# Issuing the strips of the index scores, and of their sums over heads, as one row per set

## The chip, the cores and the metric

The kernel runs on one core of one Trainium2 chip. The metric is the device time of one execution in microseconds (us). The engines that matter here are TensorE (PE in the profile, its weight loads PEld), VectorE (DVE), ScalarE (ACT), GpSimd (POOL) and SyncE (SP, which issues most of the DMAs).

## The reference

The program is one decoder layer over 512 prompt tokens and 8 sample sequences of 4 new tokens each: a SwiGLU block, a mixer (a gated convolution beside sparse attention), and a second SwiGLU block. The part in question is the indexer of the samples. For each sample it scores all 4096 cached keys, and the scores pick the 256 keys that attention may use:

```
def indexer_scores(qi, wi, ki):
    s = jax.nn.relu(jnp.einsum('bqhd,bsd->bqhs', qi, ki).astype(jnp.float32))
    return jnp.einsum('bqhs,bqh->bqs', s, wi.astype(jnp.float32)) * (D_IDX ** -0.5 * N_IDX_HEADS ** -0.5)
```

`qi` are the index queries (8 heads of 64), `ki` the cached index keys (64 wide), `wi` a weight for each head.

## The kernel before

All of it is written for one core with a tile framework. The Python code traces instructions, each with a priority; a scheduler then sets the order on each engine by these priorities and by its own estimate of when inputs are ready, and puts in the waits. Inside the mixer a planner interleaves generators ("A" and "B" for the index projections, "S" for the sample scores, "Q" and "K" for the other projections, "V" for the search of the threshold, "L" for raw logits, "D" for the prompt's top-k, and so on), and gives each a priority offset. After the second half of the first SwiGLU block ends at about 400 us, the mixer begins, and it ends at about 800 us; the second SwiGLU block follows.

`sample_scores` (generator S) does the indexer of the samples. It works in 8 steps n, 4 for each half jh of the keys; a step takes two samples (b2 = 0 and 1).

- `keys(n, b2)` gathers 512 KB of index keys into `kn` by an indirect DMA from POOL's queue (4 buffers, shared with the gathers of attention, `ckn`), and `key_transpose` turns them: 8 transposes on TensorE into the two PSUM banks of `KTp`, then one ACT copy into `kt`.
- `scores(n)` multiplies the queries with the two `kt`. There are four products (two halves of the columns, `hf`, by two samples, `b2`) of 512 columns. Each has 64 output rows, so the two samples write two strips of 64 partitions of one PSUM tile, `ssc`. ACT applies the ReLU and writes `Srel`, of which there are 4 buffers (n % 4).
- `gathered(jh, c)` runs when the four steps of a half are through, for each of two column halves c: four products `headsum` with 32 output rows each (one for each of the four `Srel` tiles) write four strips of 32 partitions of one PSUM tile, `SC`. ACT (for jh 0) or DVE (for jh 1) takes the sum to `sc`. The last step also scores the new tokens (`sxp`, `sxh`).

`KTp`, `ssc`, `sxp` and `sxh` share two PSUM buffers (tag "w", `wunit`), used in turn; `SC` has one buffer (tag "t").

When `sc` is complete, `sample_select` (generator V) searches the threshold with counts on DVE and ACT (tiles `flip`, `top`, `cand`). In the meantime TensorE works on projections (`nat`), keys and logits of attention and the convolution (`gc`, `hc`, `gb`).

All matmuls and transposes of the mixer go through the helpers `mm` (L134) and `tp` (L138), so these two lines carry most of TensorE's rows there. In the trace a float32 product has two MATMUL records: an "x2" is one strip.

Of the kernel before, what the change touches and what calls it, by code (L numbers as in the profile page):

```python
# [55 lines left out]
PINNED = 'BQK'  # L56
LGD = 2
KTB = 3
SB = 1
RSTEPS = 2  # L60
ZB = 1
# [60 lines left out]
class Trunk:  # L122
# [14 lines left out]
    def tp(self, *args):  # L137
        ins = self.nc.tensor.transpose(*args)  # L138
        return self.tc.keep_in_program_order(ins) if self.pin else ins

    def wunit(self, name):
        return self.ps.tile([128, 2, 512], F32, name=name, tag="w", bufs=2)
# [125 lines left out]
    def factors(self, srcs, nk):  # L268
# [13 lines left out]
        def parts(src, n):  # L282
            if n == 1:
                ts = [self.fp.tile([128, nk * 128], F32R, name=nm, tag=nm + "4", bufs=1) for nm in ("whi", "wlo")]
            else:
                slot, self.slot = self.slot, (self.slot + 1) % 3
                ts = [self.sp.tile([128, n * nk * 128], F32R, name=nm, tag=f"{nm}{slot}", bufs=1) for nm in ("whi", "wlo")]
            hi, lo = (t.rearrange("p (h k m) -> p h k m", h=n, k=nk) for t in ts)
            nc.scalar.activation(hi, src, AF.Copy)  # L289
            nc.vector.tensor_sub(lo, src, hi.bitcast(F32))  # L290
            return [(hi[:, h], lo[:, h]) for h in range(n)]

        p11, p12 = parts(st[0], 2)
        s12, s34 = (self.fp.tile([128, 2, nk, 128], F32, name=n, tag=n, bufs=SB) for n in ("s12", "s34"))
        for dst, a, b, op in ((s12[:, 0], a21, a22, ALU.add), (s12[:, 1], s12[:, 0], a11, ALU.subtract),
# [584 lines left out]
    def key_transpose(self, kn, name):  # L880
# [3 lines left out]
        for r in range(8):  # L884
            self.tp(wf[:, r * 128:(r + 1) * 128], kn[:, r * 128:(r + 1) * 128], self.ident)
        kt = self.ktp.tile([128, 1024], F32, name=name, tag="KT", bufs=KTB)
        self.nc.scalar.activation(kt, wf, AF.Copy)
        return kt

    def sample_scores(self, mp):  # L890

        nc = self.nc
        selb = mp.tile([128, 512], F32, name="selb", tag="flip", bufs=1)
        nc.gpsimd.tensor_copy(selb[:, 0:1], self.rn[:, 0:1])
        nc.scalar.dma_start(selb, self.i["c_late"])
        wm = mp.tile([128, 4, 2, 32], F32, name="wm")

        def head_weights():
            u = self.sunit("wsel")
            for bp in range(4):  # L900
                self.mm(u[:, bp * 8:(bp + 1) * 8], selb[:NS, bp * 128:(bp + 1) * 128], self.wi[:NS, 0, :],
                        start=True, stop=True)
            wt = mp.tile([128, 4, 8], F32, name="wt")
            nc.vector.tensor_mul(wt, u[:, :32].rearrange("p (a b) -> p a b", a=4), self.oneh[:, None, :].to_broadcast([128, 4, 8]))
            wc = mp.tile([128, 4], F32, name="wc")
            nc.vector.tensor_reduce(wc, wt, axis=AX.X, op=ALU.add)
            nc.gpsimd.memset(wm, 0.0)
            for bp in range(4):
                for jh in range(2):
                    nc.vector.tensor_scalar(wm[:, bp, jh, 16 * jh:16 * jh + 16], self.pat, wc[:, bp:bp + 1], None, op0=ALU.mult)  # L910

        def headsum(out, S, bp, jh):
            self.mm(out, wm[:, bp, jh, :], S, start=True, stop=True)

        sc = self.sc
        kts, SS = {}, {}

        def keys(n, b2):
            jh, bp = divmod(n, 4)
            b = 2 * bp + b2  # L920
            kn = self.gather(self.kvp, self.i["cache_idx_k"], 1024, self.ii[:, jh, b:b + 1], "kn", "kv", KV)
            kts[n, b2] = self.key_transpose(kn, "kt")

        def scores(n):
            bp = n % 4
            w = self.wunit("ssc")
            for hf in range(2):
                for b2 in range(2):
                    self.mm(w[64 * b2:64 * b2 + 64, hf, :], self.qbi[:, 2 * bp + b2].rearrange("p r t h -> p (r t h)"),
                            kts[n, b2][:, hf * 512:(hf + 1) * 512], start=True, stop=True)  # L930
            S = self.lgt(n % 4, "Srel")
            nc.scalar.activation(S, w.rearrange("p a b -> p (a b)"), AF.Relu)
            SS[bp] = S

        def gathered(jh, c):
            u = self.tunit("SC")
            for bp in range(4):
                headsum(u[32 * bp:32 * bp + 32, :], SS[bp][:, c * 512:(c + 1) * 512], bp, jh)
            dst = sc[:, 512 * c:512 * c + 512]
            if jh == 0:  # L940
                nc.scalar.activation(dst, u, AF.Copy, scale=IDX_SCALE)
            else:
                nc.vector.scalar_tensor_tensor(dst, u, IDX_SCALE, dst, op0=ALU.mult, op1=ALU.add)

        keys(0, 0)
        yield
        keys(0, 1)
        yield
        for n in range(8):
            if n == 2:  # L950
                head_weights()
            if n < 7:
                keys(n + 1, 0)
                yield
            if n == 4:
                gathered(0, 0)
                yield
                gathered(0, 1)
                yield
            scores(n)  # L960
            yield
            if n < 7:
                keys(n + 1, 1)
                yield
        sx = mp.tile([128, 4, NEXT], F32, name="sx")
        u = self.wunit("sxp")[:, 0, :]
        for bp in range(4):
            for b2 in range(2):
                self.mm(u[64 * b2:64 * b2 + 64, bp * NEXT:(bp + 1) * NEXT],
                                 self.qbi[:, 2 * bp + b2].rearrange("p r t h -> p (r t h)"), self.kix, start=True, stop=True)  # L970
        nc.scalar.activation(sx, u[:, :4 * NEXT].rearrange("p (a b) -> p a b", a=4), AF.Relu)
        u = self.wunit("sxh")[:, 0, :]
        for bp in range(4):
            headsum(u[32 * bp:32 * bp + 32, :NEXT], sx[:, bp, :], bp, 0)
        for c in range(2):
            yield
            gathered(1, c)
        ext = sc[:, NSEG:]
        nc.vector.scalar_tensor_tensor(ext, u[:, :NEXT], IDX_SCALE, self.valid, op0=ALU.mult, op1=ALU.mult)
        nc.vector.tensor_add(ext, ext, self.vfill)  # L980
# [719 lines left out]
```

## Time and profile before

| | |
|---|---|
| time, three runs | 1253.44, 1253.94, 1253.94 us; median 1253.94 |
| the profiled execution's own time | 1253.65 us, of which the span of the trace is 1251.9 us |
| granted TensorE clock, mean | 0.989 |
| TensorE busy, matmuls | 1192.6 us, 95% of the span |
| VectorE busy | 858.7 us, 69% |
| ScalarE busy | 544.2 us, 43% |
| GpSimd busy | 446.3 us, 36% |

The table is over the whole span, and stages with different limits lie in it. The products in question all lie between 425 and 475 us.

### The profile page before, as it was taken

Reading aid. Unit: us, or ns where it says so; the run is one execution under the profiler, and the core shown is the slowest. Engines: PE = TensorE matmul, PEld = TensorE weight load, DVE = VectorE, ACT = ScalarE, POOL = GpSimd, SP = SyncE. Lnnn points to the kernel's source line nnn. Section 1 sums busy time; section 2 is a strip of 40 time slices with the busy share of each in tenths; the row PEclk is TensorE's granted clock in tenths of the full one; section 3 lists DMA queues with packets and bytes.
Section 4 is the critical chain, followed back from the end, with each engine's and each line's share of the span. In section 5 each row is a group of like instructions: output and inputs, shape, how many; then the busy total and the mean of one; then the engine's idle time right before and its main releaser. Section 6 shows DMA issues by size and latency. Waiting matters only on the chain.

```text
span 1251.9 us, 22739 instructions
## 1 busy us (share of the span) xinstructions
PE 1192.6 (95%) x9216; PEld 1070.5 (86%) x9221; DVE 858.7 (69%) x1433; ACT 544.2 (43%) x830; POOL 446.3 (36%) x465
## 2 busy tenths in 40 slices
PE   8999999999999998899979999989989999999998
PEld 7999989999998747775667545779989999999998
DVE  6449998359965208999999753246997379845972
ACT  6224544134444455465534546335444134423432
POOL 2202651145302536665423222221650255204500
PEclk9999999999999998999998999999999999999999
DMA  8523224223331562245214544544223312432332
GB/s 239 140 68 105 73 86 134 86 69 90 94 104 59 168 199 85 65 139 169 66 58 142 163 135 140 164 136 135 77 60 110 110 55 86 123 93 71 95 86 75
DMA packets 184364, 136.08 MB, mean 109 GB/s; under 512 B 5706, under 2 KB 172434, under 8 KB 184260
## 3 DMA queue, kind: packets, MB, share of 16 engines
q1 hardware_dynamic: 171700, 91.62, 25.3%
q0 software_dynamic: 11904, 42.26, 10.5%
q8 instruction: 72, 1.18, 0.4%
q10 hardware_dynamic: 656, 0.76, 0.2%
q14 instruction: 32, 0.26, 0.1%
HBM read 131.66 MB, written 2.96 MB: 108 GB/s over the span
## 4 chain that ended last, share of the span: by engine, by line
PE 67%; DVE 22%; issue 5%; DMA 3%; ACT 2%; POOL 1%; DVEq 0%; ACTq 0%; POOLq 0%
PE Y L195 21%; PE U L372 10%; PE G L372 6%; DVE wlo L290 5%; PE Yo L134 3%; PE lg L134 3%; PE U L195 3%; PE nat L134 3%; PE KTp L138 3%; PE G L195 2%; DVE flip L1010 2%; DMA ckn<-in_cache_k,ik 1%; PE ssc L134 1%; DVE u L421 1%; PE O L134 1%
## 5 line engine op out<-in xcount | busy, mean ns | idle before, releaser
L297 POOL TENSOR_TENSOR s<-wst 128x512 f32<-128x512 f32 x68 | 98.2, 1448 | 363.7 <-DMA wst<-in_ffn_w_gate 209.0
L170 ACT ACTIVATE whi<-wst 128x1024 fp32r<-128x1024 f32 (+3 forms) x105 | 99.9, 957 | 203.9 <-PE Y L195 72.5
L195 PE MATMUL Y<-hl,whi 128*128 128x272 f32 (+2 forms) x704 | 147.8, 288 | 0.0
L195 PE MATMUL Y<-hh,whi 128*128 128x272 f32 (+2 forms) x704 | 147.6, 289 | 0.0
L195 PE MATMUL Y<-hh,wlo 128*128 128x272 f32 (+2 forms) x704 | 147.5, 288 | 0.0
L175 DVE TENSOR_TENSOR wlo<-wst,whi 128x1024 fp32r<-128x1024 f32 (+3 forms) x88 | 99.8, 1134 | 21.3 <-ACT whi L170 19.7
L195 PEld LDWEIGHTS Y<-hl,whi 128*128 128x128 f32 x704 | 111.5, 188 | 0.0
L195 PEld LDWEIGHTS Y<-hh,wlo 128*128 128x128 f32 x704 | 111.3, 188 | 0.0
L195 PEld LDWEIGHTS Y<-hh,whi 128*128 128x128 f32 x704 | 110.8, 188 | 0.0
L290 DVE TENSOR_TENSOR wlo<-wst,whi 128x1024 fp32r<-128x1024 f32 (+1 forms) x68 | 96.3, 1416 | 15.4 <-ACT whi L289 15.0
L509 DVE SCALAR_TENSOR_TENSOR x<-Y,x 128x544 f32<-128x544 f32 x46 | 33.2, 723 | 105.0 <-PE Y L195 105.0
L289 ACT ACTIVATE whi<-s 128x1024 fp32r<-128x1024 f32 x68 | 71.8, 1056 | 70.9 <-PE Y L195 29.8
L290 DVE TENSOR_TENSOR wlo<-s,whi 128x1024 fp32r<-128x1024 f32 x68 | 87.8, 1292 | 10.5 <-ACT whi L289 10.5
L372 PE MATMUL U<-xh,whi 128*128 128x272 f32 x272 | 78.5, 289 | 0.2 <-ACT m L375 0.2
L372 PE MATMUL G<-xh,wlo 128*128 128x272 f32 x272 | 78.4, 288 | 0.0
L372 PE MATMUL U<-xh,wlo 128*128 128x272 f32 x272 | 78.4, 288 | 0.0
L173 POOL TENSOR_TENSOR wlo<-wst,whi 128x1024 fp32r<-128x1024 f32 (+2 forms) x17 | 34.5, 2032 | 122.7 <-ACT whi L170 122.2
L372 PE MATMUL G<-xh,whi 128*128 128x272 f32 x272 | 78.3, 288 | 0.0
L372 PE MATMUL U<-xl,whi 128*128 128x272 f32 x272 | 78.1, 287 | 0.0
L372 PE MATMUL G<-xl,whi 128*128 128x272 f32 x272 | 78.1, 287 | 0.0
L289 ACT ACTIVATE whi<-wst 128x1024 fp32r<-128x1024 f32 (+1 forms) x68 | 57.2, 841 | 42.4 <-DMA wst<-in_ffn_w_gate 17.3
L372 PE MATMUL U<-x3h,wlo 128*128 128x272 f32 x204 | 61.4, 306 | 11.3 <-DVE wlo L290 11.3
(428 smaller groups left out, 3591.9 us busy)
## 6 DMA issues: line engine op xcount, KB each, us to landing
wst<-in_ffn_w_up SPq DMA_DIRECT2D x44, 512.0 KB, 4.3
wst<-in_ffn_w_gate SPq DMA_DIRECT2D x43, 512.0 KB, 3.8
wst<-in_ffn_w_down SPq DMA_DIRECT2D x32, 512.0 KB, 3.9
wst<-in_w_in SPq DMA_DIRECT2D x16, 512.0 KB, 3.7
wst<-in_ffn_w_down SPq DMA_DIRECT2D x16, 384.0 KB, 3.4
xin<-in_x_prompt SPq DMA_DIRECT2D x4, 512.0 KB
wst<-in_w_in SPq DMA_DIRECT2D x8, 256.0 KB, 4.9
wst<-in_w_out SPq DMA_DIRECT2D x8, 256.0 KB, 5.8
```

Source lines behind the costliest of these rows:

```text
L134: ins = self.nc.tensor.matmul(*args, **kw)
L138: ins = self.nc.tensor.transpose(*args)
L170: nc.scalar.activation(hi, st, AF.Copy)
L173: nc.gpsimd.tensor_tensor(lo, st, hi.bitcast(F32), op=ALU.subtract)
L175: nc.vector.tensor_sub(lo, st, hi.bitcast(F32))
L195: self.nc.tensor.matmul(unit[:, i, :c1 - c0], a[:, k, :], b[:, k, c0:c1], start=k == 0 and j == 0, stop=k == n - 1 and j == 2)
L289: nc.scalar.activation(hi, src, AF.Copy)
L290: nc.vector.tensor_sub(lo, src, hi.bitcast(F32))
L297: nc.gpsimd.tensor_tensor(dst, a, b, op=op)
L372: nc.tensor.matmul(out, w[:, k, :], b[:, k, :], start=k == 0 and j == 0, stop=k == nk - 1 and j == 2)
L509: nc.vector.scalar_tensor_tensor(xc, Y[:, :, :HT], 0.5, xc, op0=ALU.mult, op1=ALU.add)
L1010: V.tensor_scalar(junk, src, cand[:, k:k + 1], None, op0=ALU.is_ge, op1=ALU.add, accum_out=cnt[:, k:k + 1])
```

## The change

A new helper, `in_a_row`, takes the products of a set. It traces the one given first, and then the others with a priority raised by `RUN` and with an edge that keeps each of them behind the first on TensorE. In `scores` and in `gathered` the product that is given first is one that needs the tile that becomes ready last (`b2` = 1; the fourth `Srel`), so that the others have their inputs when it starts. Nothing is computed differently.

```
+RUN = 5000
...
+    def in_a_row(self, last, *others):
+
+
+        with self.tc.high_priority(offset=RUN):
+            with self.tc.issue_after(last().ins):
+                for f in others:
+                    f()
...
         def headsum(out, S, bp, jh):
-            self.mm(out, wm[:, bp, jh, :], S, start=True, stop=True)
+            return self.mm(out, wm[:, bp, jh, :], S, start=True, stop=True)
...
             w = self.wunit("ssc")
-            for hf in range(2):
-                for b2 in range(2):
-                    self.mm(w[64 * b2:64 * b2 + 64, hf, :], self.qbi[:, 2 * bp + b2].rearrange("p r t h -> p (r t h)"),
-                            kts[n, b2][:, hf * 512:(hf + 1) * 512], start=True, stop=True)
+
+            def part(hf, b2):
+                return lambda: self.mm(w[64 * b2:64 * b2 + 64, hf, :], self.qbi[:, 2 * bp + b2].rearrange("p r t h -> p (r t h)"),
+                                       kts[n, b2][:, hf * 512:(hf + 1) * 512], start=True, stop=True)
+            self.in_a_row(*[part(hf, b2) for hf in range(2) for b2 in (1, 0)])
...
             u = self.tunit("SC")
-            for bp in range(4):
-                headsum(u[32 * bp:32 * bp + 32, :], SS[bp][:, c * 512:(c + 1) * 512], bp, jh)
+            self.in_a_row(*[lambda bp=bp: headsum(u[32 * bp:32 * bp + 32, :], SS[bp][:, c * 512:(c + 1) * 512], bp, jh)
+                            for bp in (3, 0, 1, 2)])
```

The line numbers of the changed kernel are 1 to 10 higher (L134 becomes L135, L138 becomes L139). Three places show what the scheduler makes of it. First, TensorE after the second set of scores, in the kernel before (`ssc` scores, `SC` sums over heads, `KTp` transposes of keys, `qiT` and `kiT` transposes of the prompt's index queries and keys):

```order
L134 MATMUL ssc<-kt,qbi 64x512 x4
L138 MATMUL qiT<-main,nq 128x128 x2
L134 MATMUL SC<-Srel,wm 32x512
L138 MATMUL KTp<-main,kn 128x128 x8
L134 MATMUL SC<-Srel,wm 32x512
L138 MATMUL KTp<-main,kn 128x128 x8
L138 MATMUL kiT<-main,nk 128x128
L134 MATMUL ssc<-kt,qbi 64x512 x4
L138 MATMUL KTp<-main,kn 128x128 x8
L138 MATMUL qiT<-main,nq 128x128 x2
L138 MATMUL KTp<-main,kn 128x128 x2
L134 MATMUL SC<-Srel,wm 32x512
```

The same place in the changed kernel, a little further on:

```order
L135 MATMUL ssc<-kt,qbi 64x512 x4
L139 MATMUL KTp<-main,kn 128x128 x8
L139 MATMUL kiT<-main,nk 128x128
L135 MATMUL SC<-Srel,wm 32x512 x4
L139 MATMUL KTp<-main,kn 128x128 x8
L135 MATMUL ssc<-kt,qbi 64x512 x4
L139 MATMUL qiT<-main,nq 128x128 x2
L135 MATMUL nat<-wst,xs 32x256 x2
L135 MATMUL SC<-Srel,wm 32x512 x4
L139 MATMUL KTp<-main,kn 128x128 x16
L135 MATMUL ssc<-kt,qbi 64x512 x4
```

The four strips of the first sum stood one by one, each between transposes; now they follow each other behind the fourth set of scores. The second sum was a row of four already.

Second, TensorE at the end of the scores, in the kernel before (`sxp` and `sxh` are the scores and sums of the new tokens, `nat` and `natS` a projection of the samples):

```order
L134 MATMUL nat<-wst,xs 32x256 x4
L134 MATMUL ssc<-kt,qbi 64x512
L134 MATMUL SC<-Srel,wm 32x512
L134 MATMUL sxp<-kix,qbi 64x32
L134 MATMUL ssc<-kt,qbi 64x512
L134 MATMUL sxp<-kix,qbi 64x32
L134 MATMUL ssc<-kt,qbi 64x512
L134 MATMUL sxp<-kix,qbi 64x32
L134 MATMUL ssc<-kt,qbi 64x512
L134 MATMUL sxp<-kix,qbi 64x32 x5
L134 MATMUL natS<-part,main 32x256
```

And in the changed kernel:

```order
L139 MATMUL KTp<-main,kn 128x128 x8
L135 MATMUL nat<-wst,xs 32x256 x4
L135 MATMUL ssc<-kt,qbi 64x512 x4
L135 MATMUL sxp<-kix,qbi 64x32 x8
L135 MATMUL natS<-part,main 32x256
L139 MATMUL kiT<-main,nk 128x128
L135 MATMUL SC<-Srel,wm 32x512 x4
```

The last set of scores is a row of four, and so is the third sum, whose strips stood apart before. Of the eight sets of scores the first and the last were broken up before; of the four sums the first and the third.

Third, VectorE some 200 us later, where the order differs again: the rounds of the prompt's top-k (`MAX`, then `MATCH_REPLACE` on `pw`) stand beside work that frees PSUM for TensorE (`gc` of the convolution, and `P<-plg`, the prompt's softmax). Before:

```order
L1261 TENSOR_REDUCE rs<-sums 128x1
L1166 TENSOR_TENSOR gc<-gc,R_5251 128x272
L1122 MAX m_7652<-pw_4410 128x8
L1262 RECIPROCAL rs<-rs 128x1
L1123 MATCH_REPLACE pw_4410<-m_7652,pw_4410 128x256
L1122 MAX m_7655<-pw_4410 128x8
L1123 MATCH_REPLACE pw_4410<-m_7655,pw_4410 128x256
L1270 COPY px<-PxT 32x128
L1122 MAX m_7658<-pw_4410 128x8
L1123 MATCH_REPLACE pw_4410<-m_7658,pw_4410 128x256
L1349 ISA P,pmx<-plg,main 128x128
```

In the changed kernel:

```order
L1271 TENSOR_REDUCE rs<-sums 128x1
L1132 MAX m_7652<-pw_4410 128x8
L1272 RECIPROCAL rs<-rs 128x1
L1133 MATCH_REPLACE pw_4410<-m_7652,pw_4410 128x256
L1176 TENSOR_TENSOR gc<-gc,R_5251 128x272
L1132 MAX m_7655<-pw_4410 128x8
L1133 MATCH_REPLACE pw_4410<-m_7655,pw_4410 128x256
L1132 MAX m_7658<-pw_4410 128x8
L1133 MATCH_REPLACE pw_4410<-m_7658,pw_4410 128x256
L1280 COPY px<-PxT 32x128
L1132 MAX m_7661<-pw_4410 128x8
L1133 MATCH_REPLACE pw_4410<-m_7661,pw_4410 128x256
```

One more round of the top-k stands ahead of `gc` and of the first `P`; ahead of the third `P`, some fifteen rows on, it is one round and a `MAX` more. Between the second place and the third the order of VectorE is the same, and that of the other engines differs only in details.

## Rows read from the trace of the kernel before

**Rows 1.** Busy time by stretch; (x) counts instructions, PEclk granted clock.

```profile
core 0: us, PE busy (x) PEld busy (x) DVE busy (x) ACT busy (x) POOL busy (x), PEclk, DMA share, GB/s
425.28:475.00 49.72, 49.55 (x286) 23.71 (x285) 6.48 (x22) 28.28 (x39) 20.35 (x31) 1.00 0.57 171
482.00:660.00 178.00, 157.08 (x1075) 124.80 (x1075) 171.40 (x458) 90.13 (x148) 92.14 (x150) 0.96 0.32 97
```

**Rows 2.** Timeline, DVE and POOL: start, duration, instruction [idle before <- releaser].

```profile
471.22 0.61 POOL L756 TENSOR_TENSOR qsq<-nq 32x256 f32<-32x256 f32 x1 [4.96 <-ACT nq L842]
475.09 0.69 DVE L943 SCALAR_TENSOR_TENSOR sc<-SC,sc 128x512 f32<-128x512 f32 x1 [0.23 <-PE SC L134]
480.29 0.42 DVE L758 TENSOR_REDUCE qms<-qsq 128x4 f32<-128x256 f32 x1 [1.32 <-POOL qsq L756]
```

**Rows 3.** Timeline of PE: the sums, single strips and a row of four.

```profile
452.31 1.07 PE L134 MATMUL SC<-Srel,wm 128*32 128x512 f32 x8
453.30 2.26 PE L138 MATMUL KTp<-main,kn 128*128 128x128 f32 x16
455.49 1.04 PE L134 MATMUL SC<-Srel,wm 128*32 128x512 f32 x2
456.46 1.94 PE L134 MATMUL ssc<-kt,qbi 128*64 128x512 f32 x8
...
470.69 0.62 PE L134 MATMUL SC<-Srel,wm 128*32 128x512 f32 x1
...
471.72 0.39 PE L134 MATMUL nat<-whi,xh 128*128 128x256 f32 x1
```

**Rows 4.** Timeline of PE: the first set of scores, and the second.

```profile
425.28 1.08 PE L134 MATMUL ssc<-kt,qbi 128*64 128x512 f32 x4
...
429.62 0.24 PE L138 MATMUL kiT<-main,nk 32*128 32x32 f32 x1
...
431.87 1.09 PE L138 MATMUL KTp<-main,kn 128*128 128x128 f32 x8
432.89 1.94 PE L134 MATMUL ssc<-kt,qbi 128*64 128x512 f32 x8
434.76 0.44 PE L138 MATMUL qiT<-main,nq 128*128 128x128 f32 x2
```

**Rows 5.** Timeline of PE: the last set of scores.

```profile
463.95 1.09 PE L138 MATMUL KTp<-main,kn 128*128 128x128 f32 x8
...
465.54 1.07 PE L134 MATMUL ssc<-kt,qbi 128*64 128x512 f32 x2
466.54 1.04 PE L134 MATMUL SC<-Srel,wm 128*32 128x512 f32 x2
467.52 0.24 PE L134 MATMUL sxp<-kix,qbi 128*64 128x32 f32 x1
...
469.41 0.48 PE L134 MATMUL sxp<-kix,qbi 128*64 128x32 f32 x8
469.82 0.62 PE L134 MATMUL natS<-part,main 128*32 128x256 f32 x2
```

**Rows 6.** Timeline of ACT: copies of turned keys.

```profile
454.79 1.95 ACT L887 ACTIVATE kt<-KTp 128x1024 f32<-128x1024 f32 x2
...
465.14 1.02 ACT L887 ACTIVATE kt<-KTp 128x1024 f32<-128x1024 f32 x1 [0.60 <-PE KTp L138]
```

**Rows 7.** Timeline of DVE: one round of the prompt's top-k.

```profile
665.16 0.42 DVE L1122 MAX8 m<-pw 128x8 f32<-128x256 f32 x1
...
665.69 0.41 DVE L1123 MATCH_REPLACE8 pw<-m,pw 128x256 f32<-128x256 f32 x1
```

**Rows 8.** Timeline of PE at the wait behind those rounds.

```profile
673.10 0.39 PE L134 MATMUL hc<-xh,whi 128*128 128x272 f32 x1 [0.74 <-DVE pmx L1349]
```

**Rows 9.** Timeline of POOL: the last gather of index keys.

```profile
454.67 0.94 POOL L876 DMA_INDIRECT kn<-in_cache_idx_k,ii  x1 [3.71 <-PE KTp L138]
```

**Rows 10.** Chain that ended last: a gather that TensorE waited for.

```profile
700.74 5.30 DMA ckn<-in_cache_k,ik
```

## The prediction

> **What bounds the kernel now.** I looked first at the busy time by stretch, because the products of the change all lie in one of 50 us. From 425.28 to 475 us TensorE is busy for 49.55 of 49.72 us at the full clock, while VectorE has 6.5 us of work and ScalarE 28.3 [rows 1]. So TensorE is the limit there, and any time that its row of instructions gives up is worth looking for. From 482 to 660 us it is the other way round: VectorE is busy for 171.4 of 178 us, TensorE for 157 [rows 1]. That stretch begins with the search of the threshold, and the search needs the sums of the scores.
>
> Next I read how the one hands over to the other [rows 2]. VectorE takes the last sum at 475.09, but its first count of the search waits until 480.29 for something else too, a reduction `qms` that stands ahead of it in VectorE's queue and waits for POOL. POOL's part begins with `qsq` at 471.22, after 4.96 us of waiting for a copy of `natS`. `natS` is made by TensorE just before the last sums. Both ways into the search thus start from TensorE's end of this stretch, so that a gain there should pass to the search whole. To check that for POOL: with the sums done 6.3 us earlier, its chain would start 6.3 us earlier as well, since `natS` moves with them.
>
> Last I read TensorE's timeline product by product, to see what a strip costs. I count from one start to the next, because the durations overlap.
>
> **What a row saves.** A single strip of a sum holds TensorE from 455.49 to 456.46, 0.97 us. A row of four holds it from 452.31 to 453.30, 0.99 us [rows 3]. Four strips of 32 columns run side by side if nothing stands between them, and the three others are nearly free. The same is to be seen for two strips of scores: a record pair x2 and two strips x4 both last 1.07 to 1.08 us [rows 4, 5]. A whole set of scores in a row, four strips in two pairs, takes 432.89 to 434.76, 1.87 us, and eight transposes 431.87 to 432.89, 1.02 us [rows 4].
>
> The Trainium skill speaks against this in "TensorE: Matmul & The Clock Gate", Part 3, "What overlaps and what doesn't": weights of the next product load beside a running one only where the row groups differ. Strips of one set here differ in columns alone, so by that rule a row would be four strips one after another, some 3.9 us, and the change would give nothing. The trace disagrees with 0.99 us, but only for the rows that are there already, so I keep the rule as a rival.
>
> Now set by set, of those that the order shows broken up:
>
> - First scores: with the eight transposes that were mixed in, 425.28 to 429.62, 4.34 us [rows 4]. In rows 1.87 + 1.02 = 2.89. Saved 1.45.
> - First sum: four single strips at 0.97, 3.88 us. In a row 0.99. Saved 2.9. (The order has these four, each between transposes; one of them stands for all in rows 3.)
> - Third sum: three single strips, 2.91 us, and a fourth mixed with `sxh`, 470.69 to 471.72, 1.03 us [rows 3]. In a row 0.99, and `sxh` by itself at what eight records of `sxp` take, 469.41 to 469.82, 0.41 us [rows 5]. Saved 3.94 - 1.40 = 2.55.
> - Last scores with `sxp`: 465.54 to 469.82, 4.28 us, less the 0.98 of a sum's strip inside (466.54 to 467.52, counted above): 3.30 [rows 5]. In rows 1.87 + 2 x 0.41 = 2.69. Saved 0.6.
>
> Together 7.5 us. The other six sets of scores and the other two sums are rows already and save nothing.
>
> **What the rows cost.** A loose strip was also a filler: it stood where TensorE would have waited for ScalarE's copies. Three such waits come to light.
>
> - Before the sixth set of scores. In the kernel before, 16 transposes end at 455.49, where a strip starts; the first of the two copies that the scores need ends at about 454.79 + 1.95 / 2 = 455.8 [rows 3, 6]. Without the filler TensorE waits about 0.3 us.
> - Before the last set. It used to begin at 465.54 with the sample whose keys were ready, while the other's copy ended at 465.14 + 1.02 = 466.16 [rows 5, 6]. The row begins with that other sample. The wait is about 0.6 us.
> - With two PSUM buffers in turn, a unit of transposes (1.02 us) that follows a set of scores must wait for the ReLU (also a copy of 1.02 us, which starts 0.1 us behind the matmul). I go through the new order step by step with these durations and find a few such waits of 0.05 to 0.2 us; some of them are there now. I take 0.3 for all.
>
> That is 1.2 us, and 6.3 us are left at the end of the stretch. Bounds: if the waits vanish under other work, 7.5; if each of the eight steps waits by 0.4, 3.2 us are lost and 4.3 are left.
>
> The gathers are the other resource that must keep up. A buffer is free when its transposes are done, and the next transposes of that buffer come four units later. The last gather starts at 454.67 and its keys are used at 463.95, 9.3 us later [rows 9, 5]; a gather that TensorE does wait for shows 5.3 us [rows 10]. In the shorter stretch I find 7.5 to 9 us between the two, so nothing waits.
>
> **Behind the stretch.** From 482 to 660 us the order on VectorE is unchanged. Nothing in it is tied to a fixed time, the transfers follow their buffers, so I let it move as one by 6.3 us. At about 665 us the order differs. One round and a `MAX` more of the top-k stand ahead of the third `P<-plg`; a round is 0.42 + 0.41 us and a short value load, about 0.95, so 1.4 us in all [rows 7]. TensorE already waited there, 0.74 us for that very line before `hc` [rows 8], so what comes later on VectorE is paid by TensorE. VectorE has some idle time of its own in that place, and later it has those rounds behind it. The bounds are 0 (or a few tenths of a gain, if a round done early spares a wait later) and 1.4; I take the middle, 0.7.
>
> **Sum.** 7.5 - 1.2 - 0.7 = 5.6 us. Against the profiled execution's own 1253.65 us (1251.9 in the span, the rest around it, which does not change) that is 1248.0. That execution is 0.3 us under the median of the three runs, which is less than I can predict.
>
> **Rivals.** A measurement of this kernel tells about 0.2%, 2.5 us, from no change; faster therefore means below 1251.4.
>
> - *The gain is all kept, and the order behind helps.* The fillers cost nothing and the earlier top-k spares a wait: 1253.65 - 7.5 - 0.5 = 1245.6. For it: TensorE has small work (`kiT`, `qiT`) to put into gaps. Against it: the queue of TensorE is in order, and the two larger waits follow from rows.
> - *Part is given back behind.* The third `P` is late by the whole 1.4 and TensorE's waits in the stretch reach 3.2: 7.5 - 3.2 - 1.4 = 2.9, or 1250.8. For it: between 482 and 660 us there is a chain through VectorE, POOL and ScalarE with little slack, where small shifts can change who comes first.
> - *No change.* Either new rows run strip by strip, by the rule told above: 7.5 us are not saved, and as TensorE is then busy while it would wait, the time stays at about 1253.7. Or the search does not start earlier, because POOL's chain to `qms` takes longer when it falls beside other work: POOL is busy for only 20 of 50 us in the stretch [rows 1], which speaks against that.
> - *Slower: the gathers become the limit.* With 7.5 to 9 us between a buffer's release and its use, a gather of 5.3 us has 2 us to spare. If gathers took longer when they follow each other faster, every turn of the four buffers would wait. There are about three turns. To lose the 5.6 us and 2.5 more, each must wait 2.7 us, so a gather must take over 10 us: then about 1256.5. The point from which it decides at all is some 7.5 us. Against it: in the kernel before none of these transposes waits, and DMA is busy for 57% of the stretch [rows 1].
>
> **Chances.** The forecast, 4 to 7 us gained, 0.60. All kept, 7 us or more, 0.08. Partly given back, 2.5 to 4 us, 0.13. No change 0.12, of which the rule has 0.02. Slower 0.07. So faster 0.81, same 0.12, slower 0.07. The likeliest is 1248.0. The range reaches from 1245.0, just beyond the case where all is kept, to 1251.5, where the gain is given back to the edge of what can be measured; about 0.19 are left out, nearly all above.
>
> **What the changed profile would show.** Right: eight entries of `ssc` x8 and four of `SC` x8 on TensorE, at 1.87 and 0.99 us each from start to start; TensorE idle for 1 to 2 us between the first scores and the last sum, mostly before the sixth and the last set, released by `kt`; that stretch 43 to 44 us long instead of 49.7; the first count of the search 6 to 6.5 us earlier, about 474.5; all until 660 shifted by the same; and TensorE's wait for `pmx` before `hc` about 0.7 us longer. Wrong: rows of about 3.9 us (the rule), transposes that wait for `kn` from DMA (the gathers), or a search that starts early and a `gc` at 660 that does not. If clock or chain between 482 and 660 us come out otherwise than shifted, then my step "moves as one" has failed.

## The result, and the profile after

The changed kernel takes 1247.8 us (median of 8 runs, 1243.99 to 1251.16), the kernel before 1254.01 us in the same comparison (8 runs, 1251.67 to 1256.63). The ratio is 0.9945 with a 95% interval of 0.9932 to 0.9959: 6.9 us less by the ratio, 5.1 to 8.5 by its interval (6.2 between the medians). The forecast was 1248.0 us and 5.6 us less. The profiled execution took 1247.21 us, of which the span is 1245.4 us at a mean granted clock of 0.986.

Busy time by stretch, changed kernel, as in [rows 1]. The first row is from the first scores to the end of the last sum, 424.67 to 466.70 us:

```profile
core 0: us, PE busy (x) PEld busy (x) DVE busy (x) ACT busy (x) POOL busy (x), PEclk, DMA share, GB/s
424.67:466.70 42.03, 40.93 (x285) 22.31 (x284) 7.14 (x22) 28.24 (x39) 20.88 (x31) 1.00 0.66 203
482.00:660.00 178.00, 163.70 (x1106) 130.40 (x1106) 170.13 (x465) 92.71 (x155) 85.61 (x138) 0.95 0.31 94
```

The same work that took 49.7 us [rows 1] takes 42.0, at the same clock, and TensorE is idle in it for 42.03 - 40.93 = 1.1 us. TensorE's timeline shows the rows (start, duration, instruction; they answer to [rows 3 to 5]):

```profile
424.67 1.94 PE L135 MATMUL ssc<-kt,qbi 128*64 128x512 f32 x8
426.54 1.09 PE L139 MATMUL KTp<-main,kn 128*128 128x128 f32 x8
427.56 0.24 PE L139 MATMUL kiT<-main,nk 32*128 32x32 f32 x1
...
442.23 1.06 PE L135 MATMUL SC<-Srel,wm 128*32 128x512 f32 x8
443.23 1.09 PE L139 MATMUL KTp<-main,kn 128*128 128x128 f32 x8
...
446.50 0.64 PE L135 MATMUL SC<-Srel,wm 128*32 128x512 f32 x2
446.73 0.39 PE L135 MATMUL nat<-wst,xs 128*32 128x256 f32 x2
446.94 1.03 PE L135 MATMUL SC<-Srel,wm 128*32 128x512 f32 x6
447.90 2.27 PE L139 MATMUL KTp<-main,kn 128*128 128x128 f32 x16
450.48 1.94 PE L135 MATMUL ssc<-kt,qbi 128*64 128x512 f32 x8 [0.31 <-ACT kt L896]
...
459.31 1.94 PE L135 MATMUL ssc<-kt,qbi 128*64 128x512 f32 x8 [0.60 <-ACT kt L896]
461.08 0.61 PE L135 MATMUL sxp<-kix,qbi 128*64 128x32 f32 x16
461.61 0.62 PE L135 MATMUL natS<-part,main 128*32 128x256 f32 x2
...
462.42 1.06 PE L135 MATMUL SC<-Srel,wm 128*32 128x512 f32 x8
463.31 0.24 PE L135 MATMUL sxh<-sx,wm 128*32 128x32 f32 x8
463.48 0.39 PE L135 MATMUL nat<-whi,xh 128*128 128x256 f32 x1
...
465.71 1.06 PE L135 MATMUL SC<-Srel,wm 128*32 128x512 f32 x8
466.71 0.38 PE L135 MATMUL nat<-whi,xl 128*128 128x256 f32 x1
```

The first sum, four loose strips before, holds TensorE from 442.23 to 443.23, 1.00 us; the first scores hold it from 424.67 to 426.54, 1.87 us. The waits for ScalarE's copy of the turned keys, 0.31 us before the sixth set of scores and 0.60 us before the last, are new. The list of waits shows no others of TensorE in this stretch, none for a gather among them (what, waited for what, total, times, longest):

```profile
PE ssc L135 <- ACT kt L896: 0.9, 2, 0.6
```

VectorE and POOL, as in [rows 2], and POOL's second `qsq`, the one that `qms` waits for:

```profile
462.90 0.60 POOL L765 TENSOR_TENSOR qsq<-nq 32x256 f32<-32x256 f32 x1 [3.55 <-ACT nq L851]
466.85 0.69 DVE L953 SCALAR_TENSOR_TENSOR sc<-SC,sc 128x512 f32<-128x512 f32 x1 [0.35 <-PE SC L135]
471.27 0.60 POOL L765 TENSOR_TENSOR qsq<-nq 128x256 f32<-128x256 f32 x1
471.90 0.42 DVE L767 TENSOR_REDUCE qms<-qsq 128x4 f32<-128x256 f32 x1 [1.10 <-POOL qsq L765]
472.44 1.31 DVE L1020 TENSOR_SCALAR_CACHE_REDUCE flip<-top,cand 128x1056 uint16<-128x1056 int16 x1
```

In the kernel before, that second `qsq` stands at

```profile
479.65 0.61 POOL L756 TENSOR_TENSOR qsq<-nq 128x256 f32<-128x256 f32 x1
```

The last sum is taken at 466.85 instead of 475.09, and the first count of the search follows at 472.44 instead of 480.82: 8.4 us earlier, of which 0.6 us is from before the stretch (424.67 against 425.28). The order of waits is the old one, POOL's `qsq` last. POOL's chain moves whole: its first `qsq` from 471.22 [rows 2] to 462.90, its second from 479.65 to 471.27.

What became of it is read by comparing equal instructions in the two traces, on VectorE up to 658 us and on TensorE behind. From 482 to 490 us of before they come 8.4 us earlier, from 498 to 518 us 9.0, from 522 to 658 us about 7.8 throughout, at 673 to 700 about 8.9, at 757 5.3, and at the end 6.5. A second profiled execution of the changed kernel (the run "again" below) has 7.1 to 7.9 us from 484 to 658 us, about 7.4 from 673 to 706, and 7.8 at the end. The wait of `hc` for `pmx`, 0.74 us before [rows 8], is 1.52 us:

```profile
664.19 0.39 PE L135 MATMUL hc<-xh,whi 128*128 128x272 f32 x1 [1.52 <-DVE pmx L1359]
```

### The profile page after: what moved, and what is told of

Same layout as the page of the kernel before. It is cut to its first block, busy times and chain, and to the rows that moved or that the text cites. A ratio compares the mean times of both kernels' runs of the same rounds, so it can differ in the third digit from the quotient of the medians.

```text
span 1245.4 us, 22734 instructions
## 1 busy us (share of the span) xinstructions
PE 1189.3 (95%) x9216; PEld 1073.0 (86%) x9221; DVE 857.4 (69%) x1433; ACT 543.2 (44%) x830; POOL 446.4 (36%) x465
## 4 chain that ended last, share of the span: by engine, by line
PE 63%; DVE 25%; issue 5%; ACT 3%; DMA 3%; POOL 1%; DVEq 0%; ACTq 0%; POOLq 0%
PE Y L204 21%; PE U L381 10%; DVE wlo L299 6%; PE G L381 5%; PE Yo L135 4%; DVE flip L1020 3%; PE U L204 3%; PE lg L135 2%; PE KTp L139 2%; PE G L204 2%; PE nat L135 2%; DVE u L430 1%; DMA ckn<-in_cache_k,ik 1%; PE O L135 1%; PE ssc L135 1%
## 5 line engine op out<-in xcount | busy, mean ns | idle before, releaser
L299 DVE TENSOR_TENSOR wlo<-s,whi 128x1024 fp32r<-128x1024 f32 x68 | 87.8, 1292 | 10.7 <-ACT whi L298 10.7
```

## The experiments

Two theories stood against each other at first. *Rows*: strips in different columns run side by side only while they follow each other, and the whole gain comes from that, passed on by the search. *Order*: the raised priority also moves other work (transposes, gathers, top-k rounds), and part of the gain or loss comes from there. Each run was compared with the kernel before on its own chip (medians of before 1254.5 us in every group). Where no interval stands the differences are between medians.

**The changed kernel again**, without an edit.

> The changed kernel once more, to see what of its profile comes back. Theory (strips of a row share TensorE, the stretch of the scores shortens by 7.6 us, and some of it is lost behind 690 us to waits for gathers and a lowered clock): 1246 to 1250 us, the stretch from the first scores to the last sum again 42.0 us within 0.2, the first count of the search again near 472.4 us, while the part behind 690 us differs by a few us from the first profile. Rival (all places are as fixed as the stretch itself): the shift against the kernel before is again 8.9 us at 700 and 5.5 us at 740.

Measured: 1247.52 us, ratio 0.9943 (0.9930 to 0.9956). The stretch is 42.0 us again, with the same two waits. The first count comes at 473.74, not near 472.4, because the stretch itself begins 1.3 us later, at 425.97, behind a lowered clock (last section). The shift is 7.3 us at 700 and 8.2 at 740, not 8.9 and 5.5, so the places behind 690 us are not fixed. The wait of `hc` is 1.23 us:

```profile
665.66 0.39 PE L135 MATMUL hc<-xh,whi 128*128 128x272 f32 x1 [1.23 <-DVE pmx L1359]
```

**Scores in rows, sums as before.**

```
-            self.in_a_row(*[lambda bp=bp: headsum(...) for bp in (3, 0, 1, 2)])
+            for bp in range(4):
+                headsum(u[32 * bp:32 * bp + 32, :], SS[bp][:, c * 512:(c + 1) * 512], bp, jh)
```

> Scores in a row, sums as before the change. Theory (each broken set saves what its strips cost one by one: 1.45 us for the first scores and 0.6 for the last): 1252 us, 2 us less than before, the stretch from 49.7 to about 47.5 us. Rival 1 (the gain comes from the scheduler's new order as a whole, not from the strips): anywhere from 1247 to 1254, without relation to the broken sets that are left. Rival 2 (scores carry most of it): 1249 or less.

Measured: 1250.86 us, ratio 0.9969 (0.9956 to 0.9981). The stretch takes 45.9 us, from 424.85 to 470.77. That is 1.6 us less than expected, in part because two strips of the first sum happen to stand together here (the first of these rows has four records, two strips, in the time of the second). The time gains 3.7 us (2.4 to 5.5) where about 2 were expected:

```profile
433.98 1.05 PE L135 MATMUL SC<-Srel,wm 128*32 128x512 f32 x4
...
439.31 1.04 PE L135 MATMUL SC<-Srel,wm 128*32 128x512 f32 x2
```

**Sums in rows, scores as before.**

```
-            self.in_a_row(*[part(hf, b2) for hf in range(2) for b2 in (1, 0)])
+            for hf in range(2):
+                for b2 in range(2):
+                    self.mm(w[64 * b2:64 * b2 + 64, hf, :], ...)
```

> Sums in a row, scores as before the change. Theory: the two broken sums save 2.9 and 2.5 us, together 5.4, less about a wait of 0.3: 1249 us, the stretch about 44.5 us. Rival 1 (order as a whole): no relation. Rival 2 (scores carry most): 1252 or more.

Measured: 1249.99 us, ratio 0.9961 (0.9948 to 0.9974). The stretch takes 43.7 us, from 427.57 to 471.23; it begins 2.3 us late in the profiled execution (the clock, below). Between medians the parts give 3.7 and 4.5 us, and both together 7.0.

**Each sum as four full-width products.** The weights of each `headsum` are widened to 128 columns with zeros, and the four products are accumulated, so that the sums are the same while the strips cannot run side by side.

```
-        wm = mp.tile([128, 4, 2, 32], F32, name="wm")
+        wm = mp.tile([128, 432], F32, name="wm")
...
-            return self.mm(out, wm[:, bp, jh, :], S, start=True, stop=True)
+            return self.mm(out, wm[:, 96 * bp + 16 - 16 * jh:96 * bp + 144 - 16 * jh], S, start=bp == first, stop=bp == last)
```

> The changed kernel, with each product of a sum widened to all 128 columns by zeros, the four of a row added up in PSUM: the same sums, the same order of a row, but nothing left to run side by side. Theory: a row of a sum takes 4 x 0.98 = 3.9 us or a little less in place of 0.99, four rows lose up to 11.6 us, so 1257 to 1260 us, slower than the kernel before. Rival (what helps is that the row is not interrupted, for order, mode switches or waits; width does not matter): 1247 to 1250 us, rows near 1 us.

Measured: 1254.09 us, ratio 1.0000 (0.9988 to 1.0012): better than expected. The sum itself is as expected, 438.88 to 442.41, 3.53 us in place of 1.00:

```profile
438.88 3.70 PE L135 MATMUL SC<-Srel,wm 128*128 128x512 f32 x8
442.41 1.04 PE L139 MATMUL KTp<-main,kn 128*128 128x128 f32 x8
```

The stretch takes 52.95 us, 10.9 more than in the changed kernel (four sums at 2.53 more are 10.1). Against four loose strips, 4 x 0.97 = 3.88 us [rows 3], the uninterrupted row of full width saves 0.35 us, so by this estimate nearly all that a row saves comes from strips side by side, and little from not being interrupted. But the stretch begins 4 us earlier, at 420.70. The larger tile `wm`, cleared on POOL, made the scheduler put the third unit of turned keys later, and a wait ahead of the stretch went away. The next experiment takes this side effect by itself.

**The larger cleared tile alone.** The changed kernel, with the tile of 432 columns cleared but only the first 256 used.

```
-        wm = mp.tile([128, 4, 2, 32], F32, name="wm")
+        wmf = mp.tile([128, 432], F32, name="wm")
+        wm = wmf[:, :256].rearrange("p (a b c) -> p a b c", a=4, b=2)
...
-            nc.gpsimd.memset(wm, 0.0)
+            nc.gpsimd.memset(wmf, 0.0)
```

> The changed kernel with a longer clear of the weights' tile on POOL (432 columns, the added ones unused), which makes the scheduler put the third unit of transposes at about 405 us behind the first sums of a projection; on VectorE the order at 665 us comes out with fewer rounds ahead of the third softmax. Theory: the wait of 2.3 to 2.8 us for gathered keys at 405 us goes, and with it the lowered clock that follows it in some executions, 2.5 to 4 us: 1244 us. Rival (the wait only moves to the next transposes): 1247 to 1248.

Measured: 1243.36 us, ratio 0.9921 (0.9905 to 0.9937). With the side effect equal, the wide sums thus cost 10.7 us of time between medians (1254.09 against 1243.36), about what they add to the stretch (52.95 us against 42.6 here). Where the changed kernel waits for a gather, this one begins the unit 1.7 us earlier, at 404.07, behind `natS`, and does not wait. TensorE, third unit of keys, in the changed kernel and then with the larger tile:

```profile
405.75 1.06 PE L139 MATMUL KTp<-main,kn 128*128 128x128 f32 x8 [2.54 <-DMA kn<-in_cache_idx_k,ii]
```

```profile
404.07 1.09 PE L139 MATMUL KTp<-main,kn 128*128 128x128 f32 x8
```

The order on VectorE differs too: fewer rounds of the top-k stand ahead of the third `P`, and `hc` waits for 0.74 us as in the kernel before.

```profile
661.34 0.39 PE L135 MATMUL hc<-xh,whi 128*128 128x272 f32 x1 [0.74 <-DVE pmx L1360]
```

**The same once more, on another chip.**

> The changed kernel with the larger cleared tile once more, to compare with on the same chip: 1243.4 us, within 1.5; the first scores start at about 420.8, without a wait for a gather before them; the wait of hc for pmx is at most 0.8 us, as VectorE has fewer rounds of the top-k ahead of the third P.

Measured: 1244.25 us, ratio 0.9919 (0.9899 to 0.9939). The first scores start at 420.83 without a wait, as expected; `hc` waits for 1.14 us, more than expected, so the order on VectorE alone does not fix that wait.

**The larger cleared tile in the kernel before.** There VectorE keeps its order of rounds, so this is the later third unit without the rest.

> The kernel before with the larger cleared tile and nothing else: the scheduler puts the third unit of turned keys behind natS, as in the changed kernel with the same edit, while VectorE keeps the rounds of the top-k in the order of the kernel before, and all products are broken up as before. Theory (the wait for the gather before 406 us is worth its 2.4 us and the clock that it costs, and all moves as one): the first scores start 4 us earlier, at 421.0 to 421.5, and the time falls by as much, to about 1250 us. Rival 1: the gain of that edit came from the order of VectorE at 665 us, which here stays: 1253 to 1254. Rival 2: what is gained there is lost again behind 650 us: 1252 to 1254 with the first scores at 421.

Measured: 1251.94 us, ratio 0.9979 (0.9966 to 0.9991). The first scores start at 421.95, 3.3 us earlier than before (0.53 us of it lies ahead of the unit), the shift is 2.73 us at 434 to 473 us and 1.95 at 800. `hc` waits for 0.74 us. The time lies just below what rival 2 expected, but the lead is not lost behind 650 us: 0.6 us of it go by 434 us, and at the end it is 2.7 again. So the later unit is worth about 2.5 us, less than expected. In the changed kernel the same edit gives 3.3 to 4.2; the 1 us or so between them is as large as the difference in VectorE's order was thought to be, but the medians do not resolve it.

**No raised priority** (the edge behind the first strip stays).

```
-RUN = 5000
+RUN = 0
```

> The changed kernel with RUN = 0: the others of a set still stay behind the one given first, but without the raised priority. By the order three of the four sums are rows, the first sum is broken into two singles and a pair, and the first and the last scores are broken as before the change. Theory (time follows from the rows alone): about 2 us for the scores and 2 for the broken sum are lost against the changed kernel, the stretch takes 45 to 46.5 us, time 1251 to 1252. Rival (the edge alone does it): 1248.

Measured: 1253.33 us, ratio 0.9991 (0.9978 to 1.0005). The stretch takes 46.1 us, as expected. The first sum falls into a pair and two singles, and the first and the last scores are broken up as before, while the third sum is a row (the last line):

```profile
442.58 1.05 PE L135 MATMUL SC<-Srel,wm 128*32 128x512 f32 x4
...
443.82 1.05 PE L135 MATMUL SC<-Srel,wm 128*32 128x512 f32 x2
...
445.06 1.04 PE L135 MATMUL SC<-Srel,wm 128*32 128x512 f32 x2
...
465.18 1.07 PE L135 MATMUL SC<-Srel,wm 128*32 128x512 f32 x8
```

So the edge alone makes a row of the third sum; the first sum and the first and the last scores need the priority. The time is worse than expected. The profiled execution took 1248.49 us, the fastest of 12 (up to 1256.96), and its trace does not show what the others lost. This stays open.

**The logits of attention in rows too.** In `qk` the logits of one sample are two strips of the same 32 columns, one after the other. The edit takes two samples together and alternates them, in all eight calls.

```
+        def strips(*b4s):
+            ...
+            self.in_a_row(*[part(b4, rr) for rr in range(2) for b4 in reversed(b4s)])
...
+            if b4 == 2:
+                w = self.wunit("lg")
+                strips(0, 1)
+        yield
+        yield
+        strips(2, 3)
```

> The changed kernel, and the same helper for the logits of attention: the four strips of 32 rows are issued in two rows of two strips for each half of the columns, in place of one sample's two halves at a time. Theory (strips that follow each other in different columns share TensorE; a sample by itself takes 1.83 us, two in a row 1.85): each of the eight calls saves up to 1.8 us of TensorE. Four calls lie before 600 us, where VectorE is the limit, and give nothing; four lie between 680 and 770 us on TensorE's chain, up to 7 us, of which waits for gathered keys take some back: 1243 us, 1241 to 1246. Rival (behind 680 us the gathers set the pace, not TensorE): 1247 to 1248, no gain.

Measured: 1250.89 us, ratio 0.9963 (0.9949 to 0.9976), not 1243. Against equal instructions of the changed kernel TensorE is 0.4 us late at 558 us, 8.4 at 567 and 9.2 at 638. The order there is another: `gc` waits for a copy of `qiTs`, which it does not do in the changed kernel.

```profile
569.53 0.57 PE L135 MATMUL gc<-xh,whi 128*128 128x272 f32 x1 [5.47 <-ACT qiTs L164]
```

From 672 to 768 us, where the last four calls lie, it goes from 10.0 us late to 0.7 early; some 3.5 of these 10.7 us the changed kernel's own execution loses there (below). Behind 768 us it falls back, to 2.5 us late at 780 and 5.2 at the end.

**Both of the last edits.**

> Both of the two last at once: logits in rows and the later third unit. Theory (they lie in different stretches and add up): 1240 us, 1237 to 1243. Rival (gathers set the pace behind 680 us and take back what comes earlier): 1244 or more.

Measured: 1246.33 us, ratio 0.9945 (0.9926 to 0.9964), not 1240: 3 us slower than with the larger tile alone. The logits of the first four calls cost more than those of the last four give.

**The logits in rows in the last four calls alone**, with the larger tile. The edit is as above, under `if more:`.

> The kernel with the key turn later, and besides it the strips of the raw logits of attention in rows of two per column half, but only in the calls of the second group of samples, which lie behind 660 us; the calls before 640 us keep their old order, and so does every other engine. Theory (a row of strips of equal rows saves what its strips lasted one by one, wherever it stands; what the version with all logits lost, it lost to its order before 645 us): between 645 and 770 us the shift falls by up to 7.5 us as it did there, of which gathers of keys (5.3 us each, TensorE waits for some of them in that stretch already) give back about half: 1239 us, 1236 to 1241. Rival: what was regained there was only a delay made up for, and the stretch is set by gathers and VectorE: no gain, 1243 to 1244.

Measured: 1241.32 us, just above the expected range, ratio 0.9895 (0.9879 to 0.9911), the lowest median of the study; it runs 13.2 us below the kernel before, and 2.9 us below the version with the larger tile on the same chip. One call of logits in that version, and then in this one:

```profile
671.09 1.92 PE L135 MATMUL lg<-KT,qbd 128*32 128x512 f32 x8
672.94 0.92 PE L135 MATMUL plg<-kTs,qTs 64*128 64x384 f32 x4
673.78 1.90 PE L135 MATMUL lg<-KT,qbd 128*32 128x512 f32 x4
675.62 1.09 PE L139 MATMUL KTp<-main,ckn 128*128 128x128 f32 x8
...
678.16 1.90 PE L135 MATMUL lg<-KT,qbd 128*32 128x512 f32 x4
```

```profile
671.49 1.91 PE L135 MATMUL lg<-KT,qbd 128*32 128x512 f32 x8
673.33 0.92 PE L135 MATMUL plg<-kTs,qTs 64*128 64x384 f32 x4
...
677.57 1.91 PE L135 MATMUL lg<-KT,qbd 128*32 128x512 f32 x8
...
718.95 1.09 PE L139 MATMUL KTp<-main,ckn 128*128 128x128 f32 x8 [1.95 <-DMA ckn<-in_cache_k,ik]
...
769.65 1.09 PE L139 MATMUL PT<-main,L 128*128 128x128 f32 x8 [1.75 <-ACT PTs L1308]
```

Without the edit the third and the fourth sample take 1.84 us each (673.78 to 675.62); with it both together take about as long. A call saves up to 1.84 us; in two of the four the strips of three samples stood together already, and by the busy time of `lg` from 640 to 800 us, 23.54 against 16.80, all four save 6.7. Some 40% of it is kept, between medians. Two things take back the rest, as far as the traces show. One is late keys, as at 718.95, where TensorE waits 1.95 us for a gather (the longest such wait there was 1.06 us without the edit); but from 640 to 800 us the waits for gathers add up to 6.8 us against 6.3, so this is the smaller part. The other lies behind the last logits: by 755 us TensorE is some 5 us ahead of the version without the edit, by 780 only 2.0. There it waits 1.75 us for a copy on ScalarE, `PTs` (the last row above), which all three versions with these rows show and the versions without do not.

## Why the prediction was right

**TensorE is the limit, and the search takes over what it gives up.** Right. The first count moved by 8.4 us, and up to 658 us VectorE's work behind it by 7.8 to 9.0. Each part alone gives its share: 3.7 us for the scores, 4.5 for the sums.

**What the rows save: 7.5 us.** Right in kind, 0.8 us low. Adding up the time from each row's start to the next one's on TensorE, over the stretch, by tile:

```
tile            before   after   saved (us)
SC and sxh        9.86    4.25     5.61
ssc and sxp      17.53   15.39     2.14
KTp              14.80   14.74     0.06
nat               3.83    4.06    -0.23
all others        3.65    3.60     0.05
together         49.67   42.04     7.63
```

This is what is left with all costs in it. The prediction's four sets, as it cut them, give the saving without them:

```
set                               before   after   saved   predicted (us)
first scores with 8 transposes      4.34    2.89    1.45        1.45
first sum                           3.92    1.00    2.92        2.9
third sum with sxh                  3.95    1.06    2.89        2.55
last scores with sxp                3.30    2.30    1.00        0.6
together                           15.51    7.25    8.26        7.5
```

The difference is in the small products of the new tokens, which the prediction priced at their old 0.41 us for eight records: here `sxh` adds 0.17 us to its row (463.31 to 463.48), and sixteen records of `sxp` take 0.53 (461.08 to 461.61).

The rival by which a row would run strip by strip is refuted: 1.00 us against 3.53 for four products that cannot run side by side. The Trainium skill's rule from which that rival was drawn, in "TensorE: Matmul & The Clock Gate", Part 3, "What overlaps and what doesn't", speaks of the loading of weights alone; that products in different columns would follow one another was the prediction's own step. The trace bears out neither for these strips: they have equal rows of the array, and still four take the time of one, and all eight loads of their weights lie in the first 0.16 us of the row at 442.23:

```profile
442.23 0.16 PEld L135 LDWEIGHTS SC<-Srel,wm 128*32 128x32 f32 x8 [0.23 <-ACT Srel L942]
```

**What the rows cost: 1.2 us.** The two named waits came out at 0.31 and 0.60 us, as derived (0.3 and 0.6). The 0.3 us of further waits did not appear: TensorE is idle for 1.10 us in the stretch, 0.17 before [rows 1], and the difference is the two waits. As a term of the sum it was about twice too large. The sets above save 8.26 us and the stretch 7.63, so the rest of it costs 0.63 us, less than the two waits; transposes and projections that follow each other in longer runs made up for some 0.3. That last part is argued from the sums, not tested. So the stretch became 42.0 us long, not 43 to 44.

**The gathers keep up.** Right for the index keys: no transposition in the stretch waits for one. The rival that ended slower is refuted. Elsewhere gathers do set the pace: ahead of the stretch (2.54 us) and for some of the logits behind 690 us. The price of that rival, about 1256.5 us, is 1256.1 by its own terms (8.1 us above 1248.0), which changes nothing.

**"Moves as one" from 482 to 660 us.** Right within about 1 us: on VectorE 8.4 us, then 9.0, then 7.8 from 522 us on in one execution, 7.1 to 7.9 in the other. (In the prediction's reading 480.29 is the start of `qms`; the first count follows at 480.82. The chain is as told.)

**VectorE's order at 665 us: 0.7 us.** Right in size in both executions: `hc` waits 0.78 us longer in one and 0.49 in the other. That its cause is the extra rounds is supported: in the four traces with them ahead of the third `P` (the changed kernel's two, wide sums, no raised priority) the wait is 1.23 to 1.56 us, in the seven with fewer 0.39 to 1.14. The spread within each group shows that something else has a say.

**The sum: 5.6 us.** With 7.63 for the stretch and 0.5 to 0.8 given back, 6.8 to 7.1 us are to be expected, and the two comparisons give 6.9 (5.1 to 8.5) and 7.2 (5.5 to 8.8) by their ratios. The forecast was low by 0.8 us in what the rows save and by 0.6 in what they cost, so the stretch came out nearer to the rival by which the gain is all kept (7.5 us); the intervals do not tell 5.6 from 7.5. That 1248.0 met 1247.8 so closely is luck in part: between the medians the gain is 6.2 us, not 5.6, and the forecast was reckoned from an execution 0.4 us below the median of the comparison, which hides most of the difference. The profiled execution itself kept less, since its lead falls by some 3.5 us between 700 and 757 us, in a part of which the granted clock is below one (0.83 from 720 to 730 us); in the other execution the lead stays between 7.35 and 8.2 us.

## What to carry to other kernels

Strips that share the array's rows but not its columns are almost free beside each other, as long as nothing of full width is issued between them. Look for them in the order that the scheduler made and not in the source: here two of four sums and six of eight sets of scores were rows already, and an edge without a priority made only one more. A filler that leaves a gap can be charged by the copy that it covered (0.3 and 0.6 us, as derived), but small products that join a row need not be charged what they take alone; and an edit as small as the size of a cleared tile can move an order by more than the change in hand, so compare the orders before giving a time a cause.

## What the runs showed of the hardware

**Side by side does not seem to need strict alternation.** In the first fence on logits above, two samples in the order of the source, first, first, second, second (eight records at 671.09; a row does not name the sample), take 1.85 us, as long as the alternating order at 671.49. Two strips in the same columns with no partner take 1.84 us, twice a single strip's 0.97 [rows 3].

**The same wait costs clock in some executions and not in others.** TensorE waits 2.3 to 2.8 us for a gather before 406 us. After 2.54 us the granted clock stays at 1.00, after 2.77 us it is 0.53 in the next 7 us, and eight transposes take 1.94 us in place of 1.06, which is the lower of the two levels (1.2 and 2.4 GHz) for most of them. The changed kernel, and then the version with only the sums in rows:

```profile
405.00:412.00 7.00, 6.25 (x49) 4.67 (x50) 1.30 (x3) 2.62 (x7) 5.60 (x12) 1.00 0.86 273
```

```profile
406.12 1.94 PE L139 MATMUL KTp<-main,kn 128*128 128x128 f32 x8 [2.77 <-DMA kn<-in_cache_idx_k,ii]
...
405.00:412.00 7.00, 5.88 (x31) 3.35 (x31) 0.00 (x0) 2.08 (x5) 3.89 (x7) 0.53 0.85 283
```

The changed kernel's second execution has 0.76 there after 2.34 us, so the length of the wait does not decide it alone. The larger cleared tile takes this wait away, and in its two profiled executions the clock stays at 1.00. Later in the span, between 640 and 730 us, the places with a lowered clock differ from one execution to the next; in the same stretch the shifts scatter by 1 to 3 us, more than the term of 0.7 us that was to be found among them. That the clock is the cause of that scatter is likely, not shown.
